# Token columns sent to TensorE with the halves of a tile interleaved

## The chip, the core and the metric

The kernel runs on one core of a Trainium2 chip. The metric is the device time of one execution in microseconds (us); less is better. The engines are named as in the profile: PE is TensorE's matmul, PEld its load of weights, DVE VectorE, ACT ScalarE, POOL GpSimd, SP the engine whose queue issues most of the transfers.

## The reference

One inference step of a one-layer decoder trunk in float32, for a prompt of 256 tokens and 8 single sample tokens with states. It is cut here to the products, which are nearly all of the work:

```python
xn = rms_norm(x, g_mix)                       # (tokens, 2048)
z = xn @ w_in                                 # 2048 -> 3584, split among three mixers
y_pool = pool_mixer(z[:, :512]) @ w_pool_br   # 512 -> 2048, with 4 maps of 128 x 128
y_lru = (rg_lru(conv4(z[...])) * gelu(z[...])) @ w_lru_br    # 1024 -> 2048, 16 maps of 128 x 128
y_conf = silu(layer_norm(conv31(glu(z[...])))) @ w_conf_br   # 512 -> 2048
gates = sigmoid(xn @ w_gate + b_gate)         # 2048 -> 3 x 2048
x = x + (g_a * y_pool + g_b * y_lru + g_c * y_conf) @ w_out  # 2048 -> 2048
x = x + square(relu(rms_norm(x, g_mlp) @ w_up)) @ w_down     # 2048 -> 8192 -> 2048
y = rms_norm(x, g_final)
```

The new states of the three mixers (the last rows of their inputs, and the last hidden state) are outputs too.

## The kernel before

All activations lie with the features on the 128 partitions and the tokens along the free dimension: a tile is `[128, N]` of 4-byte words with `N = TP + TS = 256 + 8 = 264`. The first 256 columns are the prompt, the last 8 the samples, so one row of one tile is 1056 bytes. A tensor of 2048 features is 16 such tiles, one behind the other on each partition.

Each product is a **split product**. A weight and an activation are both written as a high part, rounded to float32r, and the rest, float32r as well, and a product of a 128x128 block of weights with a 128x264 tile of activations is three matmuls into the same accumulator (`mm3`, lines 150 to 153): high weight by high activation, high by low, low by high. Every matmul is an instruction of its own with its own load of weights. Accumulators are banks of PSUM, taken in turn from a pool of eight (`acc`).

The weights come from `wall`, a stream of 1 MB transfers issued on SP's queue (`dma_pair`). A chunk is 1024 words on each partition, that is two blocks of input features by 512 output features. `split` (lines 140 to 148) makes the high part of a chunk with a copy on ACT (L147) and the rest with a subtraction on DVE (L148), three chunks ahead of its use (`AHEAD`). The main loop (from line 847) walks over the chunks. `tile_mm` gives a chunk to PE: for each of its two blocks of input features and for each of four output tiles one `mm3`, so 24 matmuls for a chunk. `first_mm` (line 822) does the first block of the kernel in another order. A group is a run of 2 to 8 chunks that fills four accumulators; at its end an evacuation reads each of them into SBUF, mostly on DVE: with the factor `rstd` of the norm (`gel_evac`, `cb_evac`, `pool_evac` at L597 and L598, `gate_evac`, `up_evac`), with the gate (`branch_evac`), with the GLU's other half (`ca_evac`), or added to the residual (`out_evac`, `down_evac` at L764). The gates of the LRU and the pool's maps are evacuated on ACT (`lru_gate_mm`, `grp_mm`). Where the prompt's columns and the samples' go to different places (`lru_x_evac`, `ca_evac`, `pool_evac`), two instructions do it, of 256 and of 8 columns.

The rest (convolutions, scans, norms) is queued by hand with costs for each engine and put between the chunks by `run_bg`. At the end a matmul with a matrix of ones sums the squares (L907), ACT and DVE make the last factor (L209 to L914), and DVE and POOL scale the output, which is sent out in pieces (L918 to L923).

In `mm3` and in `first_mm` the moving operand is a plain slice `A[:, k, :]`, `L[:, ct, :]`, `Q(i)` and so on: 264 neighbouring words on each partition, read in the order of the tokens, so that column j of an accumulator is token j.

Of the kernel before, what the change touches and what calls it, by code (L numbers as in the profile page):

```python
# [11 lines left out]
AF = mybir.ActivationFunctionType  # L12
ALU = mybir.AluOpType
AX = mybir.AxisListType

P = 128
D = 2048
TP = 256
TS = 8
N = TP + TS  # L20
# [57 lines left out]
def hybrid_step(ctx: ExitStack, tc: tile.TileContext, x_in, par_in, st_in, wall, y_out, st_out):  # L78
    nc = tc.nc
# [4 lines left out]
    def f(ap):  # L84
        return ap.bitcast(F32)
# [7 lines left out]
    X = GX[:, KD:].rearrange("p (k n) -> p k n", k=KD)  # L93
# [6 lines left out]
    rstd = cpool.tile([P, N], F32, name="rstd")  # L100
# [5 lines left out]
    def pv(name, i=None, n=1):  # L106
        a, b = PCOL[name]
        return par[:, a:b] if i is None else par[:, a + i:a + i + n]
# [5 lines left out]
    pext = qtmp[:, 2900:2900 + 4 * (15 + TP)].rearrange("p (g n) -> p g n", g=4)  # L114
    vext = B[3].rearrange("p a n -> p (a n)")[:, 8 * N - 4 * (30 + TP):].rearrange("p (g n) -> p g n", g=4)
# [24 lines left out]
    def split(j, half=None):  # L140
# [6 lines left out]
        nc.scalar.copy(h[:, s], r[:, s])  # L147
        nc.vector.tensor_tensor(lo[:, s], r[:, s], f(h[:, s]), op=ALU.subtract)  # L148

    def mm3(ps, whi_t, wlo_t, xh, xl, first, last):  # L150
        nc.tensor.matmul(ps[:, :N], whi_t, xh, start=first, stop=False)  # L151
        nc.tensor.matmul(ps[:, :N], whi_t, xl, start=False, stop=False)  # L152
        nc.tensor.matmul(ps[:, :N], wlo_t, xh, start=False, stop=last)  # L153
# [47 lines left out]
    def spend(**kw):  # L201
        for e, c in kw.items():
            credit[e] -= c
# [48 lines left out]
    el = B[0].rearrange("p a n -> p (a n)")[:, :8 * (TP + 3)].rearrange("p (a n) -> p a n", a=8)  # L252
# [55 lines left out]
    st_lc = st[:, S_LC:S_LC + 256].rearrange("p (c b k) -> p c b k", c=8, b=8)  # L308
    st_cc = st[:, S_CC:S_CC + 992].rearrange("p (c b k) -> p c b k", c=4, b=8)
    st_po = st[:, S_POOL:S_POOL + 512].rearrange("p (c b k) -> p c b k", c=4, b=8)  # L310
# [3 lines left out]
    TM, GEL, RA, _ = B  # L314
# [10 lines left out]
        return slice(2 * c, 2 * c + 2)  # L325

    def lru_x_copy(ct, ps):
        nc.vector.tensor_copy(CT[:, ct, :], ps[:, :N])
        spend(dve=0.42)

    def lru_x_scale():
# [3 lines left out]
        lru_conv(range(4))  # L335

    def lru_x_evac(ct, ps):
        nc.vector.tensor_tensor(el[:, ct, 3:], ps[:, :TP], rstd[:, :TP], op=ALU.mult)
        nc.vector.tensor_tensor(st_lc[:, ct, :, 3], ps[:, TP:N], rstd[:, TP:], op=ALU.mult)
        spend(dve=0.5)  # L340

    def lru_conv(cts):
# [52 lines left out]
    def lru_gate_mm(ct, c, j):  # L395
        assert "xc" in done
        hi, lo = whi[:, c % NHI, :], wlo[:, c % NHI, :]
        out = []
        for t in range(2):
            s = slice((2 * j + t) * P, (2 * j + t + 1) * P)  # L400
            ps = acc()
            mm3(ps, hi[:, s], lo[:, s], L[:, ct, :], L[:, 8 + ct, :], True, True)
            out.append(ps)
        nc.scalar.activation(RA[:, ct, :], out[0][:, :N], AF.Sigmoid, bias=pv("b_lru_a", ct))
        nc.scalar.activation(TM[:, ct, :], out[1][:, :N], AF.Sigmoid, bias=pv("b_lru_x", ct))
        spend(act=1.0)
        if ct % 2:
            def times():
                nc.vector.tensor_tensor(XC[:, ct - 1:ct + 1, :], XC[:, ct - 1:ct + 1, :], TM[:, ct - 1:ct + 1, :],
                                        op=ALU.mult)  # L410
                spend(dve=0.71)

            later(1, times)
# [57 lines left out]

    def gel_evac(ct, ps):
        assert "conv" in done
        nc.vector.tensor_tensor(GEL[:, ct, :], ps[:, :N], rstd, op=ALU.mult)
        spend(dve=0.4)

    def gelu(c0):
# [16 lines left out]
    CT = G[:, 12:16, :]  # L494
    SG = G[:, 16:20, :]
    VC = G[:, 20:24, :]

    def cb_evac(ct, ps):
        nc.vector.tensor_tensor(SG[:, ct, :], ps[:, :N], rstd, op=ALU.mult)
        spend(dve=0.43)  # L500
        if ct == 3:
            later(1, lambda: nc.scalar.activation(SG, SG, AF.Sigmoid))
            later(2, scaled)
# [3 lines left out]
        spend(dve=1.25)  # L507

    def ca_evac(ct, ps):
        nc.vector.tensor_tensor(vext[:, ct, 30:], ps[:, :TP], SG[:, ct, :TP], op=ALU.mult)  # L510
        nc.vector.tensor_tensor(st_cc[:, ct, :, 30], ps[:, TP:N], SG[:, ct, TP:], op=ALU.mult)
        spend(dve=0.5)

    def conf():
# [79 lines left out]


    def pool_evac(gi, ps):
        nc.vector.tensor_tensor(pext[:, gi, 15:], ps[:, :TP], rstd[:, :TP], op=ALU.mult)  # L597
        nc.vector.tensor_tensor(st_po[:, gi, :, 15], ps[:, TP:N], rstd[:, TP:], op=ALU.mult)  # L598
        spend(dve=0.5)

    Sa = qtmp[:, 0:4 * W].rearrange("p (g n) -> p g n", g=4)
# [1 line left out]
    DU = G[:, 8:12, :]  # L603
# [39 lines left out]
    def grp_mm(c):  # L643
        assert "pool" in done
        hi, lo = whi[:, c % NHI, :], wlo[:, c % NHI, :]
        for gi in range(4):
            s = slice(gi * P, (gi + 1) * P)
            ps = acc()
            mm3(ps, hi[:, s], lo[:, s], Q(gi), Q(8 + gi), True, True)
            nc.scalar.activation(DU[:, gi, :], ps[:, :N], AF.Copy, scale=pv("pool_scale", gi))  # L650
        stage_split("pool", 2, lambda c: Q(slice(2 * c, 2 * c + 2)), lambda c: Q(slice(8 + 2 * c, 10 + 2 * c)), lambda c: DU[:, 2 * c:2 * c + 2, :])
        mark("pool", "grp")

# [18 lines left out]
    def gate_evac(br, g, m, ps):  # L672
        assert {"b_term", "grp"} <= done and (br != 1 or g % 2 == 0 or "lru" in done) and ("conf" in done or br < 2 or g < 3)
        t = gate_tile(br, g, m)
        nc.vector.tensor_tensor(t, ps[:, :N], rstd, op=ALU.mult)

        def rest():
            nc.scalar.activation(t, t, AF.Sigmoid, bias=pv("b_gate", br * 16 + g * 4 + m))
            spend(act=0.5)

        spend(dve=0.43)
        later(1 + m // 2, rest)

    def branch_evac(br, g, m, ps):
        assert "grp" in done and (br < 1 or "lru" in done) and (br < 2 or "conf" in done)
        t = gate_tile(br, g, m)
        k = g * 4 + m
        nc.vector.tensor_tensor(t, ps[:, :N], t, op=ALU.mult)
        spend(dve=0.43)
        if br == 1:  # L690
            nc.gpsimd.tensor_tensor(partial(k), t, gate_tile(0, g, m), op=ALU.add)  # L691
            spend(pool=0.8)
        if br == 2:
            nc.gpsimd.tensor_tensor(t, t, partial(k), op=ALU.add)
            spend(pool=0.8)
            later_split(A[:, k, :], A[:, 16 + k, :], t, 1)
# [14 lines left out]
    sq2 = G[:, 20, :]  # L711

    def out_evac(m, ps):
        nc.vector.tensor_tensor(X[:, m, :], X[:, m, :], ps[:, :N], op=ALU.add)
        spend(dve=0.4)

        hi, lo = bpart(m)

        def one():
            nc.scalar.activation(hi, X[:, m, :], AF.Copy, scale=pv("g_mlp", m))  # L720
            square_add(m)
            spend(act=0.8)

        def other():
            nc.vector.scalar_tensor_tensor(lo, X[:, m, :], pv("g_mlp", m), f(hi),
                                           op0=ALU.mult, op1=ALU.subtract)
            spend(dve=0.35)

        later(m % 4 // 2, one)
        later(m % 4 // 2 + 1, other)  # L730
        if m == KD - 1:
            later(4, lambda: rms_close(sq2))
# [12 lines left out]
    def up_evac(q, m, ps):  # L745
        hi, lo = hid(q, m)
        t = G[:, m % 8, :]
        nc.vector.scalar_tensor_tensor(t, ps[:, :N], 0.0, rstd, op0=ALU.max, op1=ALU.mult)
        spend(dve=0.4)

        def one():
            nc.scalar.activation(t, t, AF.Square)
            nc.scalar.copy(hi, t)
            spend(act=0.8)

        def other():
            nc.vector.tensor_tensor(lo, t, f(hi), op=ALU.subtract)
            spend(dve=0.35)

        later(1 + m % 4 // 2, one)  # L760
        later(2 + m % 4 // 2, other)

    def down_evac(q, m, ps):
        nc.vector.tensor_tensor(X[:, m, :], X[:, m, :], ps[:, :N], op=ALU.add)  # L764
        spend(dve=0.4)
        if q == 3:
            def rest():
                square_add(m, m < KD - 2)
                nc.scalar.activation(X[:, m, :], X[:, m, :], AF.Copy, scale=gfin[:, m:m + 1])

            later(0 if m >= KD - 4 else 1 + m % 4 // 2, rest)
# [50 lines left out]
    def first_mm(rhs, pss):  # L822
        xh, xl = rhs(0)
        for w, x, start in ((whi, xh, True), (whi, xl, False), (wlo, xh, False)):
            for m in range(4):
                nc.tensor.matmul(pss[m][:, :N], w[:, 0, m * P:(m + 1) * P], x, start=start, stop=False)  # L826

    def tile_mm(i, c, kt, m, rhs, pss, stop):
        s = slice(kt * 512 + m * P, kt * 512 + (m + 1) * P)
# [16 lines left out]
    pss = None  # L846
    for i, ch in enumerate(chunks):
# [13 lines left out]
        kind, gi, c, _ = ch  # L861
        if kind == "dense":
            rhs, fn = group(gi)
            n = groups[gi][2] // 2
            if c == 0:
                pss = [acc() for _ in range(4)]
# [38 lines left out]
    ps = acc()  # L905
# [3 lines left out]
    t = G[:, 9, :]  # L909
# [104 lines left out]
```

## Time and profile before

| what | value |
|---|---|
| device time, median of 3 runs | 1411.44 us (1411.32 to 1411.96) |
| span of the profiled execution | 1410.3 us (its own device time is not listed; the median is 1.14 us more than its span) |
| PE busy | 1396.0 us, 11418 matmuls |
| DVE busy | 830.4 us |
| ACT busy | 718.7 us |
| POOL busy | 98.0 us |
| mean granted TensorE clock | 0.997 |
| bytes moved by DMA | 256.95 MB, mean 182 GB/s |

The profile's times are of one execution. A group of instructions is given by its line in the kernel, its engine, what it writes and reads, its shape and its count, then by its busy time, the mean time of one instruction in ns, and the idle time of the engine just before with what ended it. A matmul's own mean time is longer than the distance to the next one, since matmuls overlap in the array.

### The profile page before, as it was taken

What the parts mean: (1) busy time and instruction counts of PE and PEld (TensorE: products, weight loads), DVE (VectorE), ACT (ScalarE), POOL (GpSimd) and SP (SyncE); (2) the same over time, 40 slices, a digit from 0 to 9 for tenths busy, and PEclk for the clock granted to TensorE, in tenths of its full rate; (3) what the DMA queues carried; (4) which work ended last, traced back from release to release, by engine and by line L of the source; (5) the groups of instructions that cost most, each with busy time, mean ns of one, the idle gap of its engine ahead of it and who ended that gap; (6) DMA issues with size and microseconds to landing.
All of it is one profiled execution on the core that took longest, in us unless ns stands there. A gap on an engine that the chain in (4) does not pass through costs nothing.

```text
span 1410.3 us, 26593 instructions
## 1 busy us (share of the span) xinstructions
PE 1396.0 (99%) x11418; PEld 1394.3 (99%) x11418; DVE 830.4 (59%) x1031; ACT 718.7 (51%) x1005; POOL 98.0 (7%) x122
## 2 busy tenths in 40 slices
PE   9999999999999999999999999999999999999996
PEld 9999999999999999999999999999999999999996
DVE  7685787776766648565545445544455544455443
ACT  7657576656664645454544334543344533354543
POOL 0230010110102103010000000000000000000012
PEclk9999999999999999999999999999999999999998
DMA  9455555555655554555555555555555555555551
GB/s 335 161 187 187 167 199 183 179 181 181 211 179 177 176 182 153 207 181 179 181 180 180 182 183 181 182 183 180 182 181 182 184 181 181 180 180 180 180 180 62
DMA packets 39286, 256.95 MB, mean 182 GB/s; under 512 B 4352, under 2 KB 5760, under 8 KB 9728
## 3 DMA queue, kind: packets, MB, share of 16 engines
q1 hardware_dynamic: 37872, 253.12, 52.9%
q8 instruction: 89, 1.46, 0.4%
q10 hardware_dynamic: 1152, 1.09, 0.2%
q0 software_dynamic: 144, 1.04, 0.2%
q14 instruction: 29, 0.24, 0.1%
HBM read 252.03 MB, written 3.21 MB: 181 GB/s over the span
## 4 chain that ended last, share of the span: by engine, by line
PE 98%; POOL 0%; DVE 0%; DMA 0%; ACT 0%; issue 0%; DVEq 0%; ACTq 0%
PE acc L153 33%; PE acc L151 33%; PE acc L152 32%; DMA raw<-wall_dram 0%; POOL tmp L691 0%; DVE GX L918 0%; PE acc L826 0%; ACT whi L147 0%; POOL G L543 0%; POOL G L542 0%; DVE wlo L148 0%; PE acc L549 0%; PE acc L222 0%; PE acc L907 0%; DVEq L993 0%
## 5 line engine op out<-in xcount | busy, mean ns | idle before, releaser
L148 DVE TENSOR_TENSOR wlo<-raw,whi 128x1024 fp32r<-128x1024 f32 (+1 forms) x480 | 586.8, 1224 | 551.4 <-ACT whi L147 549.8
L147 ACT CAST whi<-raw 128x1024 fp32r<-128x1024 f32 (+1 forms) x480 | 497.6, 1038 | 629.4 <-PE acc L152 576.1
L151 PE MATMUL acc<-A,whi 128*128 128x264 f32 x1980 | 564.7, 285 | 0.0
L153 PE MATMUL acc<-A,wlo 128*128 128x264 f32 x1980 | 563.4, 285 | 0.0
L152 PE MATMUL acc<-A,whi 128*128 128x264 f32 x1980 | 562.5, 284 | 0.0
L152 PEld LDWEIGHTS acc<-A,whi 128*128 128x128 f32 x1980 | 374.3, 189 | 0.1
L151 PEld LDWEIGHTS acc<-A,whi 128*128 128x128 f32 x1980 | 373.5, 189 | 0.1
L153 PEld LDWEIGHTS acc<-A,wlo 128*128 128x128 f32 x1980 | 373.5, 189 | 0.0
L151 PE MATMUL acc<-xn,whi 128*128 128x264 f32 x1024 | 291.9, 285 | 0.0
L153 PE MATMUL acc<-xn,wlo 128*128 128x264 f32 x1024 | 291.3, 285 | 0.0
L152 PE MATMUL acc<-xn,whi 128*128 128x264 f32 x1024 | 290.8, 284 | 0.0
L152 PEld LDWEIGHTS acc<-xn,whi 128*128 128x128 f32 x1024 | 193.5, 189 | 0.0
L153 PEld LDWEIGHTS acc<-xn,wlo 128*128 128x128 f32 x1024 | 193.1, 189 | 0.0
L151 PEld LDWEIGHTS acc<-xn,whi 128*128 128x128 f32 x1024 | 193.0, 189 | 0.0
L152 PE MATMUL acc<-Q,whi 128*128 128x264 f32 x644 | 182.6, 284 | 0.0
L153 PE MATMUL acc<-LH,wlo 128*128 128x264 f32 x640 | 182.3, 285 | 0.0
L151 PE MATMUL acc<-LH,whi 128*128 128x264 f32 x640 | 182.0, 284 | 0.0
L152 PEld LDWEIGHTS acc<-Q,whi 128*128 128x128 f32 x644 | 121.5, 189 | 0.0
L153 PEld LDWEIGHTS acc<-LH,wlo 128*128 128x128 f32 x640 | 120.4, 188 | 0.0
L151 PEld LDWEIGHTS acc<-LH,whi 128*128 128x128 f32 x640 | 120.4, 188 | 0.0
L738 POOL TENSOR_TENSOR G<-G 128x264 f32<-128x264 f32 x28 | 25.7, 918 | 809.9 <-ACT G L736 808.9
L524 ACT ACTIVATE G<-tmp,par 128x256 f32<-128x256 f32 x120 | 54.3, 500 | 1.7 <-DVE G L527 1.0
(171 smaller groups left out, 762.8 us busy)
## 6 DMA issues: line engine op xcount, KB each, us to landing
raw<-wall_dram SPq DMA_DIRECT2D x230, 1024.0 KB, 4.9
raw<-wall_dram SPq DMA_DIRECT2D x10, 512.0 KB, 5.5
raw<-wall_dram SPq DMA_DIRECT2D x9, 256.0 KB, 3.8
GX<-x_dram SPq DMA_DIRECT2D x6, 264.0 KB, 6.3
so_dram<-st POOLq DMA_DIRECT2D x1, 1018.0 KB, 5.7
st<-st_dram SPq DMA_DIRECT2D x1, 912.0 KB, 8.3
y_dram<-GX SPq DMA_DIRECT2D x2, 396.0 KB, 3.2
y_dram<-GX ACTq DMA_DIRECT2D x4, 132.0 KB, 2.6
```

What stands on the lines that cost most here:

```text
L147: nc.scalar.copy(h[:, s], r[:, s])
L148: nc.vector.tensor_tensor(lo[:, s], r[:, s], f(h[:, s]), op=ALU.subtract)
L151: nc.tensor.matmul(ps[:, :N], whi_t, xh, start=first, stop=False)
L152: nc.tensor.matmul(ps[:, :N], whi_t, xl, start=False, stop=False)
L153: nc.tensor.matmul(ps[:, :N], wlo_t, xh, start=False, stop=last)
L524: nc.scalar.activation(dst[:, ct, :TP], vext[:, ct, k:k + TP], AF.Copy, scale=par[:, w:w + 1])
L738: nc.gpsimd.tensor_tensor(sq2, sq2, t, op=ALU.add)
```

## The change

`mm3` and `first_mm` send the same 264 columns in another order: 0, 132, 1, 133, 2, 134 and so on. `sent` gives the view: the row of a tile as 2 halves of 132 words, with the half as the innermost index. The accumulator is written as before, one column after the other, so its column 2j now holds token j and column 2j + 1 token 132 + j. The evacuations undo it: `res` reads the accumulator as two runs of 132 columns, every second column each, and `halves` gives the SBUF operands as two runs of 132 neighbouring words. Where the prompt and the samples part, `spread` takes three instructions (132, 124 and 8 columns) in place of two. The matmuls with ones, the splits of weights and activations, all else on ACT, DVE and POOL, and all transfers stay.

```diff
+    def sent(x):
+        return x.rearrange("p (t j) -> p j t", t=2)
+
+    def halves(x):
+        return x.rearrange("p (t j) -> p t j", t=2)
+
+    def res(ps):
+        return ps[:, :N].rearrange("p (j t) -> p t j", t=2)
+
+    def spread(prompt, sample, ps, f):
+        r, h = res(ps), N // 2
+        for d, a, t in ((prompt[:, :h], r[:, 0, :], slice(0, h)), (prompt[:, h:], r[:, 1, :TP - h], slice(h, TP)),
+                        (sample, r[:, 1, TP - h:], slice(TP, N))):
+            nc.vector.tensor_tensor(d, a, f[:, t], op=ALU.mult)
+
     def mm3(ps, whi_t, wlo_t, xh, xl, first, last):
+        xh, xl = sent(xh), sent(xl)
         nc.tensor.matmul(ps[:, :N], whi_t, xh, start=first, stop=False)
         nc.tensor.matmul(ps[:, :N], whi_t, xl, start=False, stop=False)
         nc.tensor.matmul(ps[:, :N], wlo_t, xh, start=False, stop=last)
...
     def lru_x_evac(ct, ps):
-        nc.vector.tensor_tensor(el[:, ct, 3:], ps[:, :TP], rstd[:, :TP], op=ALU.mult)
-        nc.vector.tensor_tensor(st_lc[:, ct, :, 3], ps[:, TP:N], rstd[:, TP:], op=ALU.mult)
+        spread(el[:, ct, 3:], st_lc[:, ct, :, 3], ps, rstd)
...
-        nc.scalar.activation(RA[:, ct, :], out[0][:, :N], AF.Sigmoid, bias=pv("b_lru_a", ct))
+        nc.scalar.activation(halves(RA[:, ct, :]), res(out[0]), AF.Sigmoid, bias=pv("b_lru_a", ct))
...
     def down_evac(q, m, ps):
-        nc.vector.tensor_tensor(X[:, m, :], X[:, m, :], ps[:, :N], op=ALU.add)
+        nc.vector.tensor_tensor(halves(X[:, m, :]), halves(X[:, m, :]), res(ps), op=ALU.add)
...
             for m in range(4):
-                nc.tensor.matmul(pss[m][:, :N], w[:, 0, m * P:(m + 1) * P], x, start=start, stop=False)
+                nc.tensor.matmul(pss[m][:, :N], w[:, 0, m * P:(m + 1) * P], sent(x), start=start, stop=False)
```

The other evacuations change in the same two ways: those with a plain destination like `down_evac`, and `ca_evac` and `pool_evac` like `lru_x_evac`.

More of the change, by code (lines that the diff above doesn't have):

```diff
@@ L327, in lru_x_copy @@
     def lru_x_copy(ct, ps):
-        nc.vector.tensor_copy(CT[:, ct, :], ps[:, :N])
+        nc.vector.tensor_copy(halves(CT[:, ct, :]), res(ps))
         spend(dve=0.42)
@@ L403, in lru_gate_mm @@
             out.append(ps)
-        nc.scalar.activation(RA[:, ct, :], out[0][:, :N], AF.Sigmoid, bias=pv("b_lru_a", ct))
-        nc.scalar.activation(TM[:, ct, :], out[1][:, :N], AF.Sigmoid, bias=pv("b_lru_x", ct))
+        nc.scalar.activation(halves(RA[:, ct, :]), res(out[0]), AF.Sigmoid, bias=pv("b_lru_a", ct))
+        nc.scalar.activation(halves(TM[:, ct, :]), res(out[1]), AF.Sigmoid, bias=pv("b_lru_x", ct))
         spend(act=1.0)
@@ L473, in gel_evac @@
         assert "conv" in done
-        nc.vector.tensor_tensor(GEL[:, ct, :], ps[:, :N], rstd, op=ALU.mult)
+        nc.vector.tensor_tensor(halves(GEL[:, ct, :]), res(ps), halves(rstd), op=ALU.mult)
         spend(dve=0.4)
@@ L498, in cb_evac @@
     def cb_evac(ct, ps):
-        nc.vector.tensor_tensor(SG[:, ct, :], ps[:, :N], rstd, op=ALU.mult)
+        nc.vector.tensor_tensor(halves(SG[:, ct, :]), res(ps), halves(rstd), op=ALU.mult)
         spend(dve=0.43)
@@ L509, in ca_evac @@
     def ca_evac(ct, ps):
-        nc.vector.tensor_tensor(vext[:, ct, 30:], ps[:, :TP], SG[:, ct, :TP], op=ALU.mult)
-        nc.vector.tensor_tensor(st_cc[:, ct, :, 30], ps[:, TP:N], SG[:, ct, TP:], op=ALU.mult)
+        spread(vext[:, ct, 30:], st_cc[:, ct, :, 30], ps, SG[:, ct, :])
         spend(dve=0.5)
@@ L596, in pool_evac @@
     def pool_evac(gi, ps):
-        nc.vector.tensor_tensor(pext[:, gi, 15:], ps[:, :TP], rstd[:, :TP], op=ALU.mult)
-        nc.vector.tensor_tensor(st_po[:, gi, :, 15], ps[:, TP:N], rstd[:, TP:], op=ALU.mult)
+        spread(pext[:, gi, 15:], st_po[:, gi, :, 15], ps, rstd)
         spend(dve=0.5)
@@ L649, in grp_mm @@
             mm3(ps, hi[:, s], lo[:, s], Q(gi), Q(8 + gi), True, True)
-            nc.scalar.activation(DU[:, gi, :], ps[:, :N], AF.Copy, scale=pv("pool_scale", gi))
+            nc.scalar.activation(halves(DU[:, gi, :]), res(ps), AF.Copy, scale=pv("pool_scale", gi))
         stage_split("pool", 2, lambda c: Q(slice(2 * c, 2 * c + 2)), lambda c: Q(slice(8 + 2 * c, 10 + 2 * c)), lambda c: DU[:, 2 * c:2 * c + 2, :])
@@ L674, in gate_evac @@
         t = gate_tile(br, g, m)
-        nc.vector.tensor_tensor(t, ps[:, :N], rstd, op=ALU.mult)
+        nc.vector.tensor_tensor(halves(t), res(ps), halves(rstd), op=ALU.mult)
         def rest():
@@ L687, in branch_evac @@
         k = g * 4 + m
-        nc.vector.tensor_tensor(t, ps[:, :N], t, op=ALU.mult)
+        nc.vector.tensor_tensor(halves(t), res(ps), halves(t), op=ALU.mult)
         spend(dve=0.43)
@@ L747, in up_evac @@
         t = G[:, m % 8, :]
-        nc.vector.scalar_tensor_tensor(t, ps[:, :N], 0.0, rstd, op0=ALU.max, op1=ALU.mult)
+        nc.vector.scalar_tensor_tensor(halves(t), res(ps), 0.0, halves(rstd), op0=ALU.max, op1=ALU.mult)
         spend(dve=0.4)
@@ L763, in down_evac @@
     def down_evac(q, m, ps):
-        nc.vector.tensor_tensor(X[:, m, :], X[:, m, :], ps[:, :N], op=ALU.add)
+        nc.vector.tensor_tensor(halves(X[:, m, :]), halves(X[:, m, :]), res(ps), op=ALU.add)
         spend(dve=0.4)
```

## The prediction

> **What bounds the kernel now.** I read the page first, for who is busy and which chain ended last.
>
> ```profile
> span 1410.3 us, 26593 instructions
> PE 1396.0 (99%) x11418; PEld 1394.3 (99%) x11418; DVE 830.4 (59%) x1031; ACT 718.7 (51%) x1005; POOL 98.0 (7%) x122
> ...
> PE 98%; POOL 0%; DVE 0%; DMA 0%; ACT 0%; issue 0%; DVEq 0%; ACTq 0%
> ```
>
> The first line is the span, the second the busy times, the last the share of each engine in the chain that ended last. PE holds 98% of that chain, and it runs from one end to the other: the time is the number of matmuls by their distance. Busy shares can't give the distance, since matmuls overlap, so next came PE's work in stretches (length, busy time and number of matmuls, granted clock) and the timeline at both ends of the stream.
>
> ```profile
> core 0: us, PE busy (x), PEclk, DMA share, GB/s
> 5.62:9.08 3.46, 3.46 (x15) 1.00 1.06 382
> 9.24:13.00 3.76, 3.76 (x33) 1.00 1.05 376
> 600.00:800.00 200.00, 200.00 (x1643) 1.00 0.54 181
> 800.00:1000.00 200.00, 200.00 (x1645) 1.00 0.54 182
> ```
> ```profile
> 5.62 2.12 PE L826 MATMUL acc<-A,whi 128*128 128x264 f32 x8 [0.78 <-ACT whi L147]
> ...
> 8.42 0.42 PE L151 MATMUL acc<-A,whi 128*128 128x264 f32 x1
> 8.64 0.42 PE L152 MATMUL acc<-A,whi 128*128 128x264 f32 x1
> 8.86 0.42 PE L153 MATMUL acc<-A,wlo 128*128 128x264 f32 x1
> ...
> 1396.70 0.28 PE L153 MATMUL acc<-LH,wlo 128*128 128x264 f32 x1
> 1396.82 1.91 PE L907 MATMUL acc<-G,ones 128*128 128x264 f32 x6
> ```
>
> In the steady stream a matmul of 264 columns follows the last one after 200 / 1645 = 121.58 ns. The first ones follow each other after 220 ns (8.42, 8.64, 8.86), and 220 / 264 = 0.833 ns for each column. From there the stream goes to 122 ns within a us. The clock column says 1.00 in both stretches, so the profile doesn't show what makes the first slow. If the array ran at half speed there, 110 ns would be its time at full speed, and 11.6 ns of the 121.58 would be something else: the row can't say whether that is the read of the moving operand, the load of weights or the step between instructions.
>
> [...]
>
> Last, the groups kept apart by shape give the count.
>
> ```profile
> L248 PE MATMUL acc<-ones 128*128 128x128 f32 x16 | 3.8, 431 | 1.1 <-DVE eps L244 1.1
> L907 PE MATMUL acc<-G,ones 128*128 128x264 f32 x6 | 1.8, 403 | 0.1
> L549 PE MATMUL acc<-G,ones 128*128 128x264 f32 x4 | 1.3, 412 | 0.8 <-POOL G L543 0.8
> L222 PE MATMUL acc<-G,ones 128*128 128x264 f32 x4 | 1.2, 386 | 0.0
> ```
>
> These 30 are not split products. 11418 - 30 = 11388 matmuls are, and all of them are changed.
>
> **The sum.** 11388 x 121.58 ns = 1384.6 us. What is left of the span is 1410.3 - 1384.6 = 25.7 us: 5.6 us before the first product, 13.5 us from 1396.82 to the end, and 6.6 us of slow start, matmuls with ones and short waits. The median, 1411.44 us, lies 1.14 us above the span of the profiled execution. So the time is 26.9 us + 11388 x distance, and each ns on the distance is 11.4 us.
>
> **The moving operand.** This is the term that decides. Nothing is added to PE's queue; but each of the 264 columns now lies 528 bytes ahead of or 524 bytes behind the one before it, where they were neighbours. No matmul of before does that, so the cost must be bounded by other rows.
>
> From below: a matmul whose operand is read as fast as now has 121.58 ns. Nothing excludes that it falls to the array's own 110 ns, if the 11.6 ns are a cost of reading neighbours.
>
> From above, and across engines: DVE's few instructions whose words lie apart.
>
> ```profile
> L338 DVE TENSOR_TENSOR tmp<-acc,rstd 128x256 f32<-128x256 f32 x4 | 1.6, 414 | 0.0
> L632 DVE TENSOR_TENSOR G<-qtmp 128x16 f32<-128x16 f32 x4 | 0.7, 176 | 0.1
> L635 DVE SCALAR_TENSOR_TENSOR G<-G,st 128x8 f32<-128x8 f32 x4 | 0.7, 173 | 0.1
> L631 DVE SCALAR_TENSOR_TENSOR qtmp<-par,qtmp 128x16 f32<-128x16 f32 x4 | 0.7, 169 | 0.0
> L598 DVE TENSOR_TENSOR st<-acc,rstd 128x8 f32<-128x8 f32 x4 | 0.6, 160 | 0.0
> L333 DVE TENSOR_TENSOR st<-G,rstd 128x32 f32<-128x32 f32 x1 | 0.2, 217 | 0.0
> L539 DVE TENSOR_TENSOR G<-G,par 128x32 f32<-128x32 f32 x1 | 0.2, 193 | 0.0
> ```
>
> Neighbouring words cost (414 - 176) / 240 = 0.99 ns each (L338 against L632). L333 writes 32 words 16 bytes apart, L539 writes 32 in runs of 8: 24 ns more, or 0.75 ns for each word, 1.74 ns in all. L635 reads one source 64 bytes apart; from L631's 169 ns for 16 words, 8 neighbouring ones would take 161, so 12 ns are too much, 1.5 ns for each word, 2.5 ns in all. Against both stands L598: 8 words written 64 bytes apart take 160 ns, no more than neighbours would. These are differences of a few ns on short instructions, of another engine, two of the three for writes. As prices of a column they give 264 x 0.99 = 261 ns, 264 x 1.74 = 459 ns and 264 x 2.5 = 660 ns for a matmul.
>
> I take 0.833 ns for a column, from PE's own row at 8.42 us, with half of the 11.6 ns added: 220 + 5.8 = 225.8 ns. The reason: in the steady stream PE gets its columns at twice that rate, 264 words in little more than 110 ns, and the simplest way to halve it is that words come in pairs and one of each pair is now thrown away. PE's own row is the nearer one, and the lowest DVE price, 261 ns, lies close to it. The ends for this case are 220 and 231.6 ns (none or all of the 11.6 ns on top). The sum: 11388 x 225.8 ns = 2571.4, + 26.9 = **2598.3 us**; the ends are 2505.4 + 26.9 = 2532.3 and 2637.3 + 26.9 = 2664.2 us.
>
> [...]
>
> **The evacuations.** 268 accumulators are read by DVE and 20 by ACT, now every second column. No row shows such a read. If it is at the full rate it costs nothing. If it costs what L635's apart words cost, it is 264 x 1.5 ns = 0.40 us each, 268 x 0.40 = 107 us more on DVE. The 12 evacuations of `spread` get one instruction more, by L598 with its 8 words some 0.16 us of fixed cost each, 1.9 us in all.
>
> ```profile
> L148 DVE TENSOR_TENSOR wlo<-raw,whi 128x1024 fp32r<-128x1024 f32 (+1 forms) x480 | 586.8, 1224 | 551.4 <-ACT whi L147 549.8
> ...
> L764 DVE TENSOR_TENSOR GX<-GX,acc 128x264 f32<-128x264 f32 x64 | 23.3, 422 | 8.2 <-PE acc L153 8.2
> ```
>
> This is hidden: DVE idles 551.4 us before its splits (L148), waiting for ACT's half of the same split, and the splits run three chunks ahead, 3 x 24 x 0.12158 = 8.8 us. Queued behind a longer evacuation on DVE are the next split and the next subtraction, and PE is the one who would wait. Four longer evacuations are at most 1.6 us against those 8.8. Without that cover the 107 us would count in full; with a slower PE the cover grows. One evacuation lies on the path: the last L764, before the last sum of squares, so 0 to 0.4 us there. I take 0, since a longer distance between matmuls dwarfs it.
>
> Transfers, splits and POOL lose nothing: they are issued as before, and a slower PE takes their results later. Nothing else becomes late; PE stays 98% or more of the chain.
>
> **The rivals.**
>
> *Four words at a time.* If the read fetches four neighbouring words at once, and 110 ns is just what that gives, then one useful word of four makes a matmul 4 x 110 = 440 ns; L333's price, 459 ns, is right beside it. For it: two DVE rows with 0.75 and 1.5 ns extra for a word. Against: L598, and that DVE is another reader. Time: 11388 x 440 ns = 5010.7, + 26.9 = 5037.6 us, to 5227.1 + 26.9 = 5254.0 us with 459 ns.
>
> [...]
>
> *No effect.* If the reader holds two lines, or fetches ahead far enough, then two neighbouring streams read in turn cost what one does. For it: both halves are still read in order, and L598 shows no cost. Then the distance stays and only the tail of the evacuations counts: 1411.4 to 1411.8 us. That the access is not what it says can be left out: 132 and 1 as steps can't be joined into one run.
>
> [...]
>
> *Faster.* If the 11.6 ns above 110 come from fetching one line right after its neighbour, and 528 bytes (33 x 16) put the two halves in memories that work side by side, then the distance falls towards 110 ns: 11388 x 110 = 1252.7, + 26.9 = 1279.6 us. It decides as soon as the distance is below 121.58 by 0.25 ns. For it: 11.6 ns that the array doesn't need. Against: PE's load of weights is as busy (1394.3 us) and could as well be what sets 121.58 ns, and the distance is the same in stretches with different tiles.
>
> *Between, and beyond.* A partial cost, a few ns to 80, gives 1450 to 2350 us. L635's 660 ns gives 7516.1 + 26.9 = 7543 us.
>
> **How the numbers follow.** Half the rate 0.42, four words at a time 0.25, no effect 0.12, faster 0.08, between 0.08, beyond 0.05. The forecast is the likeliest, 2598.3 us, with 2532 to 2664 as its own range. To hold 8 in 10, the range must reach from no effect to four words at a time: 0.12 + 0.08 + 0.42 + 0.25 = 0.87, from 1409 us (no effect with some scatter) to 5260 us. The sign is surer than the size: faster by over 0.2% 0.08, within 0.2% (about what a measurement here can tell from no change, 2.8 us) 0.12, slower 0.80.
>
> **What would show it.** In the stretch of PE's work in mid kernel, the number of matmuls in 200 us: 1645 now, about 886 by the forecast, 455 by the first rival, 1645 and 1818 by the others. In the groups, L764's mean against 422 ns for the strided read of the accumulator. In the chain, PE at 98 to 99%, and the idle time of DVE and ACT grown by about the whole difference. The forecast is wrong if the distance is not within 220 to 232 ns, and its ground is wrong if another engine shows up in the chain.

## The result and the profile after

The changed kernel takes 1310.25 us (median of 4 runs, 1309.99 to 1310.37) against 1411.38 us: a ratio of 0.9283, with a 95% interval of 0.9269 to 0.9296. It is faster by 101 us, where 2598 us were forecast.

The page of the changed kernel: span, busy times, and the engines' shares in the chain that ended last.

```profile
span 1308.2 us, 26621 instructions
PE 1291.0 (99%) x11418; PEld 1287.9 (98%) x11418; DVE 830.6 (63%) x1043; ACT 715.3 (55%) x1005; POOL 97.3 (7%) x122
...
PE 95%; DVE 2%; ACT 1%; issue 1%; POOL 0%; DMA 0%; DVEq 0%; ACTq 0%; POOLq 0%
```

PE's work in mid kernel (length, busy time and matmuls, granted clock, DMA share, GB/s), and the group of the last evacuations, L764 before:

```profile
800.00:1000.00 200.00, 200.00 (x1781) 1.00 0.58 195
```
```profile
L780 DVE TENSOR_TENSOR GX<-GX,acc 128x264 f32<-128x264 f32 x64 | 23.3, 423 | 7.3 <-PE acc L172 7.3
```

A matmul now follows the last one after 200 / 1781 = 112.30 ns, 9.28 ns sooner than the 121.58 of before, at the same granted clock. (Such a count takes in matmuls that overlap the ends of the 200 us, since one lasts 285 ns before and 276 ns after by its own mean, so both distances read some 0.2 ns low; from start to start, as in the experiments below, they are 121.7 and 112.5 ns.) That is 11388 x 9.28 ns = 105.7 us. The accumulator read in every second column costs nothing: 423 ns against 422. That the whole gain lies in the order of the moving columns is tested below. Some 4.6 us of the 105.7 don't show in the time. The rest of the span, which was 25.7 us, is 1308.2 - 11388 x 0.1123 = 29.3 us, 3.6 us more. The last us comes from setting medians against single executions: the spans of the two profiled executions lie 102.1 us apart, the medians 101.1. PE's waits show most of the 3.6 us (who waited for whom: us in total, times, longest):

```profile
PE acc L172 <- DVE wlo L148: 1.8, 3, 0.8
PE acc L566 <- POOL G L560: 1.6, 1, 1.6
```

The first was not there before, the second was 0.8 us. The faster stream catches up with the split weights three times, and it waits longer for a sum on POOL.

### The profile page after: what moved, and what is told of

Read it like the earlier page. It is cut to its first block, busy times and chain, and to the rows that moved or that the text cites. A ratio compares the mean times of both kernels' runs of the same rounds, so it can differ in the third digit from the quotient of the medians.

```text
span 1308.2 us, 26621 instructions
## 1 busy us (share of the span) xinstructions
PE 1291.0 (99%) x11418; PEld 1287.9 (98%) x11418; DVE 830.6 (63%) x1043; ACT 715.3 (55%) x1005; POOL 97.3 (7%) x122
## 4 chain that ended last, share of the span: by engine, by line
PE 95%; DVE 2%; ACT 1%; issue 1%; POOL 0%; DMA 0%; DVEq 0%; ACTq 0%; POOLq 0%
PE acc L172 32%; PE acc L171 32%; PE acc L170 31%; DVE wlo L148 1%; DVE A L720 0%; ACT tmp L372 0%; ACT whi L147 0%; DVE G L375 0%; DMA GX<-x_dram 0%; DVE GX L934 0%; POOL tmp L707 0%; DVE G L704 0%; POOL G L559 0%; DVE qtmp L166 0%; PE acc L566 0%
## 5 line engine op out<-in xcount | busy, mean ns | idle before, releaser
L172 PE MATMUL acc<-A,wlo 128*128 128x264 f32 x1980 | 547.0, 276 | 1.9 <-DVE wlo L148 1.8
L170 PE MATMUL acc<-A,whi 128*128 128x264 f32 x1980 | 547.1, 276 | 0.0
L171 PE MATMUL acc<-A,whi 128*128 128x264 f32 x1980 | 546.8, 276 | 0.1
L170 PE MATMUL acc<-xn,whi 128*128 128x264 f32 x1024 | 282.8, 276 | 0.0
L171 PE MATMUL acc<-xn,whi 128*128 128x264 f32 x1024 | 282.6, 276 | 0.0
L172 PE MATMUL acc<-xn,wlo 128*128 128x264 f32 x1024 | 282.6, 276 | 0.0
L171 PE MATMUL acc<-Q,whi 128*128 128x264 f32 x644 | 177.7, 276 | 0.0
L170 PE MATMUL acc<-LH,whi 128*128 128x264 f32 x640 | 176.6, 276 | 0.0
L172 PE MATMUL acc<-LH,wlo 128*128 128x264 f32 x640 | 176.6, 276 | 0.0
L171 PEld LDWEIGHTS acc<-Q,whi 128*128 128x128 f32 x644 | 121.7, 189 | 0.0
```

## The experiments

Eight questions, ten runs. In the runs with many patterns, each pattern holds for a group of 192 matmuls of `w_up` and one of `w_down`. A row below is one group of `w_down`, from the start of its first matmul to the start of its last, so its length divided by 191 is the distance. (The count in brackets takes in neighbours that overlap its ends.) Each of these runs is a single execution; the two groups of a pattern agree within 1.5% wherever no wait and no change of clock falls into one of them. A line, here and in the prediction's rivals, means 16 bytes of a partition's row, that is four words, so a row of a tile is 66 lines. (That the read goes by such lines is the author's working assumption; what bears it out here is that 256 neighbours take 118.5 ns from the start of the row and 117.5 ns from four words on, against 120.6 and 119.9 ns from one and two words on.) Two things are read in turn when a column comes from the one, the next column from the other, and so on.

### Which orders are fast

```diff
+ORDERS = [("plain", 264), ("turn", 2, 132), ("turn", 6, 44), ("turn", 4, 66), ("turn", 8, 33), ...]
     def mm3(ps, whi_t, wlo_t, xh, xl, first, last):
+        xh, xl = sent(xh), sent(xl)      # "turn": "p (t j) -> p j t"; "block": "p (b t j) -> p b j t", t=2
+        n = cols(xh)                     # "runs": "p (t j e) -> p j t e", t=2; "gap": two runs of 128
```

> Sixteen orders of the moving columns in one run, each for one group of w_up and one of w_down (192 split products each); evacuations read in accumulator order, so tokens are mixed up and the output is not the reference's. In brackets the words from one column to the next. Theory NEIGHBOURS (a matmul loses some 9 ns because words of the same 16-byte line or 8-byte pair follow each other): 112 ns for every order that changes the line with each column (halves +132, sixths +44, quarters +66, eighths +33, 22 runs +12, 66 runs +4, lines of a block in turn +4), 121.6 ns for neighbours and for whole lines in turn (runs of 4), between them for pairs in turn (runs of 2) and +2. Theory SIDE BY SIDE (two halves lie in memories that work at the same time): it depends on the distance, so 132 words (33 lines, odd) is at 112 ns and 128 words (32 lines, even) is slow, 121.6 ns or more. Theory FORM (a pattern of two levels is handled in another way, whatever its order): also the two runs of 128 neighbours with a gap of 4 between them fall from the time of 256 neighbours (about 118) to that of the halves (about 109). Theory HALF RATE for close words: +4 at 220 ns.

The rows, in this order: neighbours; halves in turn; 256 neighbours; two runs of 128 with a gap; 256 columns as halves 128 words apart; blocks 0, 2, 1, 3; blocks 0, 4, 1, 5, 2, 6, 3, 7; pairs of words in turn from the halves; single words 4 apart; single words 12 apart.

```profile
core 0: us, PE busy (x), PEclk, DMA share, GB/s
750.87:774.19 23.32, 23.32 (x193) 1.00 0.50 165
774.32:795.80 21.48, 21.48 (x193) 1.00 0.57 187
1541.45:1564.09 22.64, 22.64 (x193) 1.00 0.56 190
1585.65:1608.36 22.71, 22.71 (x194) 1.00 0.58 190
1564.22:1585.54 21.32, 21.32 (x193) 1.00 0.56 191
1408.14:1431.39 23.25, 23.25 (x193) 1.00 0.52 169
1431.51:1453.00 21.49, 21.49 (x193) 1.00 0.56 187
1350.63:1383.16 32.53, 32.53 (x193) 1.00 0.43 146
1156.70:1202.55 45.85, 45.85 (x192) 0.96 0.27 92
1094.83:1156.38 61.55, 61.55 (x192) 0.53 0.20 69
```

Divided by 191: 122.1, 112.5, 118.5, 118.9, 111.6, 121.7, 112.5, 170.3, 240.1 and 322.3 ns. FORM falls: the two runs with a gap are a pattern of two levels and take what neighbours take. SIDE BY SIDE falls: 128 words (an even number of lines) and 4 words apart are as fast as 132. NEIGHBOURS falls too: single words from a new line each time take 240 ns, not 112. HALF RATE comes near for these, with 220 ns. What the fast orders of this run (111.6 to 112.5 ns) have in common is two lines read in turn, four words from each; 2 apart, in one line, does nothing (121.7 against 122.1 ns). In the last row the granted clock fell, to 0.53 on average, but that doesn't make its time: the fall came some 4 us after its start, and the distances before it were 310 to 325 ns already. Whole lines in turn gave 129 ns, quarters 142.8, sixths 153.4 and eighths 231 ns.

### Columns and weights

```diff
+ORDERS = [("plain", 264), ("plain", 224), ..., ("part", 112), ..., ("shift", 1), ("wplain", 264), ("wturn", 2)]
+        if ORDERS[pat[0]][0][0] == "w":
+            s = slice(kt * 512 + m, kt * 512 + 512, 4)     # weights 4 words apart
```

> The number of columns of a matmul is varied in one run: neighbours at 264, 224, 192, 160, 128 and 96 columns and halves in turn (132 words apart) at the same numbers, each for one group of w_up and one of w_down; then 256 neighbours that begin 1 or 2 words into the row, and weights read 4 words apart with neighbours and with halves in turn. Leaves out columns, so the output is not the reference's. If the 9.3 ns are a cost for each column or line, the gap between the two orders shrinks with the number of columns (at 128: 4.5 ns). If they are a fixed cost of an instruction, it stays at 9.3 ns. If the weight load sets the distance with neighbours (about 121.6 ns whatever the number of columns), neighbours stay at 121.6 ns down to 96 columns, and halves in turn fall to the same floor. A start inside a line: no change if the cost is in the line as such, some ns if a line that is cut matters. Weights 4 words apart: no change if weights and moving words are read independently, a larger distance if they get in each other's way.

Neighbours at 224, 128 and 96 columns; then weights 4 words apart with neighbours and with halves in turn:

```profile
759.91:781.23 21.32, 21.32 (x194) 1.00 0.58 185
928.08:949.37 21.29, 21.29 (x193) 1.00 0.59 195
949.48:984.71 35.23, 35.23 (x193) 0.59 0.38 134
1419.65:1464.35 44.70, 44.70 (x193) 1.00 0.30 102
1464.59:1509.19 44.60, 44.60 (x192) 1.00 0.00 1
```

From 224 down to 128 columns both orders take 111.6 ns, and with weights 4 words apart both take 234 ns. So there is a floor of 111.6 ns, the same at all these numbers of columns. Most likely it is the weight load, since weights read 4 words apart lift it to 234 ns for both orders; whether reading weights and reading columns disturb each other this run doesn't show, since the floor of 234 ns covers the columns. The weight load was not what held neighbours at 121.6: with the same load they fell to 111.6 ns at 224 columns. At 264 columns halves in turn are 0.9 ns above this floor: there is next to nothing left to win by order. The gap between the orders at fewer columns was covered by the floor, so this run could not tell a fixed cost from one for each line. 256 neighbours that start 1 or 2 words into a line take 120.6 and 119.9 ns, some 2 ns more than the 118.5 of those that start with the row.

### The evacuations alone

```diff
     def mm3(ps, whi_t, wlo_t, xh, xl, first, last):
-        xh, xl = sent(xh), sent(xl)
...
-                nc.tensor.matmul(pss[m][:, :N], w[:, 0, m * P:(m + 1) * P], sent(x), start=start, stop=False)
+                nc.tensor.matmul(pss[m][:, :N], w[:, 0, m * P:(m + 1) * P], x, start=start, stop=False)
```

> The changed evacuations alone: columns are sent in token order as before, and the accumulators are read as after the change, so tokens are mixed up and the output is not the reference's. If the whole gain is in the order of the moving columns: 1411 to 1412 us, as before, L764's counterpart at 422 ns, 121.6 ns for a matmul. If the evacuations had a part in it: faster than before by up to 101 us.

1412.11 us, a ratio of 1.0005 (0.9995 to 1.0014); the evacuations' mean is 423 ns, and PE's stretch in mid kernel is that of before:

```profile
800.00:1000.00 200.00, 200.00 (x1644) 1.00 0.54 180
```

The evacuations have no part in the gain, and cost nothing that can be measured; the whole gain is in the order of the moving columns.

### A cost for each matmul, or for each line

```diff
+        if o[0][0] == "x":
+            at = (2 * c + kt) * N
+            xh, xl = (A.rearrange("p a n -> p (a n)")[:, b + at:b + at + o[1]] for b in (0, 15 * N))
```

> Sixteen more patterns in one run, each for one group of w_up and one of w_down; some read 320 to 512 columns (on past the end of a tile) in place of 264, and tokens are mixed up, so the output is not the reference's. First, wide matmuls: neighbours and halves in turn at 320, 384, 448 and 512 columns, where the weight load's 111.6 ns can't cover anything. The runs before left open whether neighbours cost a fixed 9 ns for each matmul or something for each line. Theory FIXED: neighbours minus halves is 9 ns at all four. Theory PER LINE (9.1 ns for 66 lines): it grows from 11 ns at 320 to 17.7 ns at 512 columns. Second, orders of 264: runs of 12 in turn from the halves, and blocks whose two halves of 3, 6, 12, 44 and 66 words are read in turn. Theory TWO LINES (two lines read in turn, four words from each, are what makes it fast): 112.5 ns for 12 and 44 words apart, which are whole lines; 3 and 6 apart, where the two words often share a line or a line is left early, between 112.5 and 121.7 or above; runs of 12, where lines follow each other, at about 121.6 ns or above. Theory FIRST LINES (only the start of a matmul matters, where two lines are asked for at once): runs of 12 and 3 apart as neighbours, all blocks from 6 on at 112.5. Third, 256 neighbours that begin one line into the row: 118 ns; 2 x 130 columns with the second half beginning inside a line: 112 ns if only the number of lines in turn matters.

320 columns as neighbours and as halves in turn, 512 in the same two ways; then blocks with 3 and with 6 words from one to the next:

```profile
998.81:1026.78 27.97, 27.97 (x192) 1.00 0.44 151
1463.97:1489.91 25.94, 25.94 (x192) 1.00 0.48 161
1099.44:1143.69 44.25, 44.25 (x192) 1.00 0.27 95
1557.57:1598.79 41.22, 41.22 (x192) 1.00 0.00 1
1236.41:1263.19 26.78, 26.78 (x193) 1.00 0.51 175
810.47:831.96 21.49, 21.49 (x193) 1.00 0.54 191
```

Halves in turn take 135.8 and 215.8 ns, which is a column at (215.8 - 135.8) / 192 = 0.417 ns with 2.5 ns on top (320 x 0.4167 + 2.5 = 135.8). Neighbours take 146.4 and 231.7 ns: the gap grows from 10.6 to 15.9 ns, so FIXED falls and PER LINE is near. It is better put as a time for each line: (231.7 - 121.6) / (128 - 66 lines) = 1.78 ns, with 4.4 ns on top, which gives 146.5 ns at 320 columns. Four columns at 0.417 ns take 1.67 ns, so neighbours would wait some 0.11 ns for each line; that is an estimate from the two fits, and no trace shows such a wait by itself. FIRST LINES falls too, since the gap grows with the columns. TWO LINES held for 12 and 44 apart (112.5), and runs of 12 took 127 ns; 6 apart was faster than it said (112.5), 3 apart slow (140). 256 neighbours that begin one whole line into the row took 117.5 ns, as expected, and 2 x 130 columns 111.7, which is the floor and so tells nothing.

### Words that are held

```diff
+        if k == "line again":
+            return x[:, None, 0:n].to_broadcast([P, N // n, n])
+        if k == "word again":
+            return x[:, 0:N // n, None].to_broadcast([P, N // n, n])
+        if k == "run of 4, step":
+            return x[:, 0:N // 4 * n].rearrange("p (a b) -> p a b", b=n)[:, :, 0:4]
```

> Sixteen reads that no product needs, in one run, each for one group of w_up and one of w_down, 264 columns each; words are repeated or taken from a wider stretch, so the output is not the reference's. It asks what costs time in the read of neighbours, and what happens without turns. Repeated words: one word 264 times, one line (4 words) 66 times, two lines one after the other 33 times, two lines in turn 33 times, three lines 22 times, each word twice, each word 4 times, each line twice. Theory NEW LINE (going on from one line to the next costs, 0.14 ns for each of 66): one word and one line again and again at 112.5 ns; two lines one after the other near 121.6; two lines in turn, each word twice (33 lines) between or at 112.5. Theory SAME LINE (a word asked for while its line is still in use by the one before costs, new or not): one word and one line again and again at 121.6 ns or more, two lines in turn at 112.5. Straight steps without turns: runs of 4 with a step of 8, runs of 2 with a step of 4, single words with steps of 2, 3, 4, 8 and 16, and two tiles in turn (264 words apart). If it is lines in a row that cost: runs of 4 at 121 to 129 ns, single words of step 4 to 16 at about 240 ns, as the +4 of the first run, step 2 at 236, two tiles in turn at 112.5.

One line again and again; two lines one after the other, again and again; each word twice; runs of 4 in steps of 8; runs of 2 in steps of 4; single words in steps of 4; two tiles in turn:

```profile
757.54:779.15 21.61, 21.61 (x193) 1.00 0.57 192
779.26:800.89 21.63, 21.63 (x193) 1.00 0.56 193
1228.43:1249.92 21.49, 21.49 (x193) 1.00 0.57 192
982.26:1005.21 22.95, 22.95 (x192) 1.00 0.50 168
1005.32:1050.29 44.97, 44.97 (x193) 1.00 0.29 101
1095.75:1141.59 45.84, 45.84 (x192) 1.00 0.27 92
1599.85:1621.36 21.51, 21.51 (x192) 1.00 0.00 1
```

113.1, 113.3, 112.5, 120.2, 235.4, 240.0 and 112.6 ns. SAME LINE falls: one line again and again costs nothing (113.1 ns). NEW LINE missed in one place. It gave two lines one after the other, again and again, some 121.6 ns, and they took 113.3; three lines took 113.4. So going on to another line cost nothing here where that line had been read shortly before, with two lines and with three (113.3 and 113.4 ns against 113.1 for one). Such lines are called held below; what holds them, and how, no trace shows. Lines that aren't held do cost: 121.6 ns for 66 in a row, 120.2 for 66 with every second one left out. Runs of 2 were the surprise: 132 lines there cost as much as 264 lines as single words. Single words 2 and 3 apart took 235.6 and 234.4 ns, 8 and 16 apart 225.5 and 225.6. That would fit columns that are taken two at a time, with one wait for a pair, whether it needs one line (runs of 2, 235.4 ns) or two (single words 4 apart, 240.0); this is a guess from the distances, and the next run tests it.

### Pairs, or single lines

```diff
+        if k == "again":
+            return x[:, 0:N // r * n:n][:, :, None].to_broadcast([P, N // r, r])
+        if k == "streams":
+            return x[:, 0:2 * r].rearrange("p (t j) -> p j t", t=2)[:, 0:N // 2 * n:n, :]
```

> Eight reads of 264 columns, each for one group of w_up and one of w_down, chosen to tell two readings of the earlier runs apart; words are repeated or taken from a wider stretch, so the output is not the reference's. Theory PAIRS: columns go two at a time; a pair that needs lines not held fetches them together in one step of 1.78 ns, steps can't overlap, and a matmul takes the larger of its columns at 0.417 ns with 2.5 ns added and its steps at 1.78 ns with 4.4 ns added. (Both constants from neighbours at 264 and 512 columns, 121.6 and 231.7 ns for 66 and 128 lines.) Theory SINGLE: every line costs 0.91 ns by itself (240 ns for 264 lines), held ones nothing. In the order of the run, PAIRS against SINGLE: words 4 apart, each twice (132 lines, 132 steps): 239 against 120 to 125 ns. Each 4 times (66 lines, 66 steps): 121.6 against 112.5. Each 6 times (44): 112.5 for both. Words 8 apart, each 8 times (33): 112.5 for both. Two streams in turn with words 2 apart (132 lines, 66 steps): 121.6 against 120 to 125. Two streams in turn with words 4 apart (264 lines, 132 steps): 239 against 240. Runs of 6 in steps of 8 (88 lines, 88 steps): 161 against 112.5. Runs of 8 in steps of 12 (66 lines, 66 steps): 121.6 against 112.5.

Words 4 apart, each twice; each 4 times; two streams with words 2 apart; with words 4 apart; runs of 6 in steps of 8:

```profile
946.16:991.16 45.00, 45.00 (x193) 1.00 0.30 104
991.39:1014.48 23.09, 23.09 (x192) 1.00 0.49 168
1366.10:1388.60 22.50, 22.50 (x193) 1.00 0.52 181
1388.71:1433.54 44.83, 44.83 (x193) 1.00 0.28 103
1433.78:1463.72 29.94, 29.94 (x192) 1.00 0.41 141
```

235.6, 120.9, 117.8, 234.7 and 156.8 ns against 239, 121.6, 121.6, 239 and 161 by PAIRS; the other three gave 112.8, 112.5 and 121.2 against 112.5, 112.5 and 121.6. All eight are within 4% of PAIRS. SINGLE missed by half on the first and falls. As an estimate, PAIRS gives both sides of the change: for neighbours a step for each line, 66 x 1.78 + 4.4 = 121.9 ns (121.6 measured), a step being 1.78 ns where four columns are 1.67; for halves in turn one step for two lines, with eight columns, 3.33 ns, before the next, so 33 x 1.78 + 4.4 = 63.1 ns, well covered by the columns' 264 x 0.4167 + 2.5 = 112.5 (112.5 measured). The steps themselves show in no trace; PAIRS is a rule worked out from distances. Some of the earlier orders it doesn't fit: single words 8 or 16 apart took 225.5 ns where it gives 239, words 12 apart 322 for the same 239, whole lines in turn 129 for 121.6, and pairs of words in turn 170.3, also for 121.6 if both lines stay held. How long a line is held is open.

### The whole kernel with lines 16 bytes apart

```diff
     def sent(x):
-        return x.rearrange("p (t j) -> p j t", t=2)
+        return x.rearrange("p (b t j) -> p b j t", t=2, j=4)
...
     def res(ps):
-        return ps[:, :N].rearrange("p (j t) -> p t j", t=2)
+        return ps[:, :N].rearrange("p (b j t) -> p b t j", t=2, j=4)
```

> The whole computation, with another order that also reads two lines in turn: in each block of 8 words 0, 4, 1, 5, 2, 6, 3, 7, so the two lines are 16 bytes apart in place of 528; evacuations undo it, up_evac with two instructions in place of one. If two lines in turn are the cause and not the distance of the halves: 112 to 113 ns for a matmul and 1308 to 1314 us. If the distance matters: nearer to 1411 us.

1310.17 us, a ratio of 0.9286 (0.9273 to 0.9299), and 1780 matmuls in 200 us. The distance of the two lines is free as far as it was tried: 16, 24, 528 and 1056 bytes gave 112.5, 112.5, 112.5 and 112.6 ns, and 512 bytes 111.6 ns for 256 columns.

### The waits that came back

```diff
-            later_split(A[:, k, :], A[:, 16 + k, :], t, 1)
+            later_split(A[:, k, :], A[:, 16 + k, :], t, 2)
...
-        stage(q, "pool", 2.0, [lambda: total(VC)], 2)
+        stage(q, "pool", 2.0, [lambda: total(VC)], 3)
```

> The changed kernel with two steps put one chunk later: the splits of the last branch's results (later_split from 1 to 2), and the second step after the sum over channels of the conformer's norm (gap of total(VC) from 2 to 3). In the changed kernel PE waits 1.1 us at 523 us, where splits stand behind casts that wait for POOL, and 1.9 us at 410 us, where the matmul with ones waits for POOL. If these waits are what the faster stream ran into: both go, and the time falls by 1 to 2.7 us to about 1308 us. If another step is late right behind: no change.

1307.25 us, a ratio of 0.9267 (0.9254 to 0.9280). Its interval overlaps the changed kernel's, so both were run again on one chip.

> The changed kernel itself, on the same chip as the next one: 1310 us.

> The changed kernel with the two steps one chunk later, on the same chip as the changed kernel: 2 to 3 us less than that, about 1307 us, if the two waits were the price that its faster stream paid; the same if the difference before came from the chip.

The changed kernel took 1310.96 us (1310.02 to 1311.36), a ratio of 0.9286 (0.9274 to 0.9299) to the kernel before; the one with later steps took 1307.21 us (1307.15 to 1307.57), a ratio of 0.9263 (0.9251 to 0.9276). The intervals of the ratios still touch, but the slowest of the one lies 2.4 us below the fastest of the other. The span of the kernel with later steps and its list of PE's waits:

```profile
span 1305.4 us, 26625 instructions
```
```profile
PE acc L267 <- DVE eps L263: 1.1, 1, 1.1
PE acc L172 <- DVE wlo L148: 1.0, 2, 0.8
PE acc L842 <- ACT whi L147: 0.3, 1, 0.3
```

The wait for POOL is gone, and one of the three for split weights. This is the fastest version: 3.75 us, 0.3%, below the changed kernel by the medians. About 3 us of that are the two steps. From start to start of PE's matmuls they took away 1.9 us at 410 us and 1.0 us at 523 us, about as much as the 2.8 us between the spans of 1308.2 us (the first profile of the changed kernel) and 1305.4 us. The remaining us is scatter: three of the five runs of the changed kernel on this chip took 1311.0 to 1311.4 us, the other two 1310.0, and the profiled one, at 1311.36 us, waited 1.3 us longer in its first 16 us, for its inputs and the first split weights, which the two steps don't touch. The waits left, at 61 and 84 us, stand behind the conv's sums on DVE. That these couldn't be put later without making the LRU's gates late is argued, and was not tried.

## Why the prediction was wrong

**What bounds the kernel** was right: 11388 products by their distance, 11.4 us for each ns. With the measured 112.30 ns the sum gives 26.9 + 1278.9 = 1305.8 us, 4.4 us below the median: the 3.6 us by which the rest of the span grew, most of them the waits above, and 0.9 us from setting medians against single executions.

**The moving operand** is the step that failed, by sign and size: 225.8 ns were taken, 112.3 measured. The step's reason, that words come in pairs and one of each is thrown away, prices a read that never comes back to a line. The change isn't such a read. It comes back to each line three more times, with one word of the other line in between, at no cost that the distance shows (112.5 ns, 0.9 above the floor), and this wasn't weighed in the forecast, though the rival of no effect had it. Reads that don't come back cost near what was given, 225.5 to 240.0 ns for single words 4, 8 and 16 apart against 220 to 231.6, but the reason isn't borne out by that: runs of 2 in steps of 4, where both words of a pair are used, took 235.4 ns, and single words 12 apart 322. There the number was near by luck. The prices from DVE's rows (261 to 660 ns) said nothing about it.

**The 11.6 ns** were left open between the read, the weight load and the step between instructions, with half of them kept in the forecast. At 264 columns 9.1 of them go with the order of the columns (121.6 - 112.5) and 2.5 stay in every order that was fast. The 110 ns, a condition in the prediction, came out: between 320 and 512 columns halves in turn pay 0.417 ns for each column, and 264 x 0.417 = 110.

**Faster**, the rival with a chance of 0.08, named the term: reading one line right after its neighbour costs (121.6 ns), two in turn don't (112.5). Its condition, memories that work side by side, showed in no run: 16, 24, 512, 528 and 1056 bytes apart are alike, at 111.6 to 112.6 ns. It was also 30.7 us too low. Its 110 ns lacked the 2.3 ns that remain (26 us), and its fixed 26.9 us the 4.4 us that came back.

**Four words at a time** had the line's size right: a start one line into the row costs nothing (117.5 against 118.5 ns), a start 1 or 2 words into a line some 2 ns (120.6 and 119.9). But even reads that use one word of each line took 225.5 to 322 ns and not 440, which PAIRS, with its one step for two lines, comes near (239), except for the 322; and the change, which uses four words of each, isn't such a read.

**The evacuations** were sized right at the lower end: 0, with 423 ns against 422. The cover was never needed. That nothing else becomes late was argued for a slower PE; for the faster one it was wrong by the waits above, and the chain shows it, with PE at 95% in place of 98.

**The range**, 1409 to 5260 us, stopped at no effect, and left out the one side on which the surplus over 110 ns could be won back, which the prediction had given 0.08.

## What to carry to other kernels

Where matmuls run back to back, set the measured distance against the columns at the rate that wider matmuls show (0.417 ns each here, from 320 and 512 columns), and take a surplus of some ns as a term to be won, whose owner can be found by varying the columns, the order and the weight load one at a time. With 264 4-byte moving words read in a row, the distance was 121.6 ns, with two lines of 16 bytes read in turn 112.5, some 0.14 ns less for each of the 66 lines; DVE and ACT undid the order at no cost that could be measured (423 ns for an evacuation against 422, and a ratio of 1.0005 for the evacuations alone). After a gain on the bounding engine, look for the steps that were only just in time: two of them, put one chunk later, gave some 3 us more.

## What the runs showed that had not been expected

The granted clock fell in two kinds of rows, on average to 0.59 with 96 columns and to 0.53 with words 12 apart (0.96 in the row after that). At 0.417 ns a column, 96 columns are 40 ns of the floor of 111.6 (at the lower clock a matmul took 184.5 ns), and 264 are 110 of 322 ns. With 128 columns, 53 of 111.6 ns, it kept 1.00. PE shows no idle time in any of these rows. What makes the clock fall was not sought, and no run shows it. Left open are the orders that PAIRS doesn't fit, or not without knowing how long a line is held: quarters 142.8, sixths 153.4, eighths 231, pairs in turn 170.3, whole lines in turn 129, blocks with words 3 apart 140 and single words 12 apart 322 ns are told of here, but not explained.
